# First loads of a two-layer decoder trunk spread over two DMA queues, small inputs packed, modulation products placed before the rotary angles

## The chip, the cores and the metric

One core of a Trainium2 chip runs the whole program. The metric is device time in microseconds for one execution. TensorE is called PE below, VectorE DVE, ScalarE ACT, GpSimd POOL, and SyncE SP; SP computes nothing here and only issues DMA transfers.

## The reference, cut to what matters

The kernel computes a decoder trunk of two layers on 256 tokens of width 1024. Layer 0 mixes tokens with multi-head latent attention with a rotary key, layer 1 with a block-sparse attention; each mixer is followed by a gated FFN. All six modulation vectors of a layer come from one vector c. What matters here is the very start:

```
ang = positions[..., None] * inv_freq ; cos, sin = cos(ang), sin(ang)
c_act = silu(c)
mod = (c_act @ mod_w[i] + mod_b[i]).reshape(B, 6, D)
hin = x * (1.0 + mod[:, 1]) + mod[:, 0]
proj = hin @ mla_w_in        # then q, k, v from proj; cos and sin turn the rotary parts
```

Before the first product of the mixer can run, a block of 128 features needs its shift and scale, that is two products of c_act with 1024x128 weights, and its part of x. Everything is float32.

## The kernel before, in words

Features lie on the 128 partitions, so x is held as z, 128 partitions by 8 blocks by 256 tokens. The modulation products aren't made on PE: `cb` holds c_act, repeated on every partition, and one VectorE instruction per half multiplies a 128x1024 slab of transposed modulation weights by it and sums along the row (`mod_half`, line 227). One unit of such weights is 1 MB and holds two halves; the first eight units (scale and shift of the first sub-layer for blocks j = 0 to 7) are loaded into tiles named `early`, the eighth into one named `raw`.

All DMA transfers are issued by SP, in one queue, in the order of lines 406 to 441: c (`cc`), the positions repeated on all partitions (`posi`), two constants of the rotary angles (`cst_sb`), modulation unit 0, the first two blocks of x, all small parameters (`par_sb`, 170 KB), a quarter of the mixer's input weights (`iraw`), unit 1, the other six blocks of x, the positions as a column (`posci`), and then the other units and quarters by turns. Unit 7 is loaded as two halves. The program keeps one completion counter for each of eight transfers in turn, so the issue of a transfer waits until the one eight places before it has landed.

The instructions of each engine run in the order in which the program writes them down (class `InOrder`). Around the change that order is: ACT takes exp(-c) (line 506), DVE finishes silu, PE transposes it eight times into PSUM (tile `cps`), ACT and DVE each copy a half to `cb` (lines 507 to 514). DVE then makes `kn2` from `par_sb` (line 552) and the first part of the rotary angles (`next(angles)`, line 564: `posb` from `posi`, `ang`, three steps on `n`). Then the loop of line 565 runs over the eight blocks j:

```
for n in range(2):
    mod_half(j, early[j], n)
...
V.tensor_add(gb0[:, :, j], modc[:, 0, 0:2, j], mb0[:, :, j])
A.activation(hin[:, j], z[:, j], AF.Identity, scale=..., bias=...)
A.mul(r[:, j], z[:, j], ALPHA)
for i in range(5): T.matmul(...)          # cqp, ckp, krp
...
next(angles, None)
```

In j = 0 four additions on `par_sb` are made, in j = 1 three products `lnx` and the copy `posc`; `next(angles, None)` makes one further part of the angles behind each of the first blocks. So PE's ten products of a block wait for ACT's `hin`, which waits for DVE's `gb0`. After the loop come the norms of the latents, the low-rank products (`wuqr`, `wuqn`, `wuk`, `wuv`), the heads and so on; from there PE works nearly without a gap, and DVE and ACT fill their idle time with splitting weights and with the remaining modulation units. What they fill in, and where, is decided while the program is built, by a model of the engines' times (class `Clock`), which also books each transfer on one data line in the order of the program.

Of the kernel before, what the change touches and what calls it, by code (L numbers as in the profile page):

```python
# [12 lines left out]
F32 = mybir.dt.float32  # L13
F32R = mybir.dt.float32r
BF16 = mybir.dt.bfloat16
I32 = mybir.dt.int32
AF = mybir.ActivationFunctionType
ALU = mybir.AluOpType
PSUM = bass.MemoryType.PSUM

P = 128
D = 1024
S = 256
NJ = D // P
# [6 lines left out]
ROPE_BASE = 10000.0  # L31
# [18 lines left out]
OFF_CB = OFF_CW + 2 * 3 * NF  # L50
OFF_QN = OFF_CB + 2 * NF
OFF_KN = OFF_QN + 2
NPAR = OFF_KN + 2

# [94 lines left out]
class InOrder:  # L151
# [6 lines left out]
    def __getattr__(self, name):  # L158
        f = getattr(self.engine, name)

        def call(*args, **kw):
            c = self.clock
            outs = [args[0]] + [kw[k] for k in ("accum_out",) if kw.get(k) is not None]
            ins = [a for a in list(args[1:]) + [v for k, v in kw.items() if k != "accum_out"] if hasattr(a, "ap")]
            size = math.prod(k for _, k in outs[0][:].ap)
            outs, ins = ([a[:] for a in x if a[:].tensor.name in c.written] for x in (outs, ins))
            if self.idle is not None:
                self.idle(c.ready(outs, ins))
            b = f(*args, **kw)  # L169
            if self.last is not None:  # L170
                self.tc.add_manual_dep(
                    b.ins, self.last.name,
                    mybir.DependencyInfo(mybir.DependencyClass.NoSync, mybir.DependencyReason.DATA),
                    reason="issue order")
            self.last = b.ins
            t = max(c.free[self.key], c.ready(outs, ins))
            if self.key == "Q":
                c.free["Q"] = t + 0.45
                c.run("D", max(c.free["Q"] + 0.65, c.free["D"]), size / 90e3, outs, ins, 1.0)
            else:  # L180
                c.run(self.key, t, c.cost(self.key, name, outs[0], ins), outs, ins)
            return b
        return call


@with_exitstack
def trunk_kernel(ctx: ExitStack, tc: tile.TileContext, xT, c_col, pos_row, pos_col, par, cst, mod,
                 w_mla_in, w_uqn, w_uqr, w_uk, w_uv, w_mla_o, w_qk, w_v, w_moba_o, w_f1, w_f2, out):
    nc = tc.nc
    clock = Clock()  # L190
    V, A, T, Q = (InOrder(tc, e, clock, k) for e, k in
                  ((nc.vector, "V"), (nc.scalar, "A"), (nc.tensor, "T"), (nc.sync, "Q")))
# [9 lines left out]
    one = ring("one", 1)  # L202
# [5 lines left out]
    psm = ring("psm", 3, space=PSUM)  # L208
# [8 lines left out]
    cb = one.tile([P, NJ, P], F32, name="cb")  # L217
# [179 lines left out]

    cc = one.tile([P, NJ], F32, name="cc")  # L400
    posi = tmp.tile([P, S], I32, name="posi", tag="t")
    posci = one.tile([P, 2], I32, name="posci")
    cst_sb = one.tile([P, 2], F32, name="cst_sb")
    par_sb = one.tile([P, NPAR], F32, name="par_sb")
    z = one.tile([P, NJ, S], F32, name="z")
    Q.dma_start(cc, c_col)
    Q.dma_start(posi, pos_row.to_broadcast([P, S]))
    Q.dma_start(cst_sb, cst)
    early, iraw = {}, {}

    def load_mod(j):
        if j < PIECES:
            early[j] = wts.tile([P, 2 * HALF], F32, name="early", tag="wx")
        else:
            early[j] = raws.tile([P, 2 * HALF], F32, name="raw", tag="raw")
        if j < NJ - 1:
            Q.dma_start(early[j], mod[j])
        else:
            for p in range(2):
                Q.dma_start(early[j][:, p * HALF:(p + 1) * HALF], mod[j][:, p])  # L420

    def load_in(k):
        iraw[k] = raws.tile([P, 2, 576], F32, name="iraw", tag="raw")
        Q.dma_start(iraw[k], w_mla_in[k])

    load_mod(0)
    Q.dma_start(z[:, 0:2], xT[:, 0:2])
    Q.dma_start(par_sb, par)
    load_in(0)
    load_mod(1)  # L430
    Q.dma_start(z[:, 2:8], xT[:, 2:8])
    Q.dma_start(posci, pos_col)
    load_mod(2)
    load_in(1)
    load_mod(3)
    load_mod(4)
    load_in(2)
    load_mod(5)
    load_mod(6)
    load_in(3)  # L440
    load_mod(7)

    def settled(li, pp):
        def still():
# [33 lines left out]
    ident = one.tile([P, P], F32, name="ident")  # L478
# [23 lines left out]
                        fill=MASKED, base=0, channel_multiplier=1)  # L502


    ce = one.tile([P, NJ], F32, name="ce")
    A.activation(ce, cc, AF.Exp, scale=-1.0)
    V.tensor_scalar(ce, ce, 1.0, None, op0=ALU.add)
    V.reciprocal(ce, ce)
    V.tensor_mul(ce, ce, cc)
    for hf in range(2):  # L510
        ps = psm.tile([P, 4, P], F32, name="cps", tag="mm")
        for j in range(4):
            T.transpose(ps[:, j], ce[:, 4 * hf + j:4 * hf + j + 1].to_broadcast([P, P]), ident)
        (A.copy if hf == 0 else V.tensor_copy)(cb[:, 4 * hf:4 * hf + 4], ps)


    hin = act.tile([P, NJ, S], F32, name="hin", tag="hh")
# [9 lines left out]
    def rotary():  # L527

        ang = tmp.tile([P, S], F32, name="ang", tag="g")
        V.tensor_copy(posb, posi)  # L530
        V.tensor_scalar(ang, posb, cst_sb[:, 0:1], None, op0=ALU.mult)
        for dst, turn, quarter in ((sin_t, 0.0, 0.0), (cos_t, 0.25, math.pi / 2)):
            n = tmp.tile([P, S], F32, name="n", tag="t")
            V.tensor_scalar(n, ang, INV_2PI, turn, op0=ALU.mult, op1=ALU.add)
            V.tensor_scalar(n, n, MAGIC, None, op0=ALU.add)
            V.tensor_scalar(n, n, MAGIC, None, op0=ALU.subtract)
            yield
            V.scalar_tensor_tensor(dst, n, -PI2_A, ang, op0=ALU.mult, op1=ALU.add)
            V.scalar_tensor_tensor(dst, n, -PI2_B, dst, op0=ALU.mult, op1=ALU.add)
            V.scalar_tensor_tensor(dst, n, -PI2_C, dst, op0=ALU.mult, op1=ALU.add)  # L540
            if quarter:
                V.tensor_scalar(dst, dst, quarter, None, op0=ALU.add)
            V.tensor_scalar(dst, dst, PI_SAFE, -PI_SAFE, op0=ALU.min, op1=ALU.max)
            A.activation(dst, dst, AF.Sin)
            yield
        A.mul(sin_t, sin_t, cst_sb[:, 1:2])
        table(AF.Abs_reciprocal_sqrt, cos_t)
        yield

    angles = rotary()  # L550
    kn2 = one.tile([P, 2], F32, name="kn2")
    V.tensor_scalar(kn2, par_sb[:, OFF_KN:OFF_KN + 2], -0.5, None, op0=ALU.mult)


    wuqr = act.tile([P, 2, 512], F32, name="wuqr", tag="k", bufs=1)
# [5 lines left out]
    Q.dma_start(wuqr, w_uqr)  # L561
    Q.dma_start(wuqn, w_uqn)
    mb0 = par_sb[:, OFF_MODB:OFF_MODB + 2 * NJ].rearrange("p (a j) -> p a j", a=2)
    next(angles)
    for j in range(NJ):
        k = j % 2
        raw = iraw[j // 2]
        if k == 0:
            krw = tmp.tile([P, 2, 2, 64], F32, name="krw", tag="krw", bufs=1)
            G.tensor_copy(krw, raw[:, :, 512:576].unsqueeze(2).to_broadcast([P, 2, 2, 64]))  # L570
        for n in range(2):
            mod_half(j, early[j], n)
        (wts if j < PIECES else raws).done.add(early[j][:].tensor.name)
        if j == 0:
            for li in range(2):
                for p_ in (1, 4):
                    V.tensor_scalar(modb(li, p_), modb(li, p_), 1.0, None, op0=ALU.add)
        if j == 1:
            lg = par_sb[:, OFF_LNG:OFF_LNG + 4 * NJ].rearrange("p (n j) -> p n j", n=4)
            lb = par_sb[:, OFF_LNB:OFF_LNB + 4 * NJ].rearrange("p (n j) -> p n j", n=4)  # L580
            V.tensor_scalar(lnx[:, 0], lb, ALPHA, None, op0=ALU.mult)
            V.tensor_scalar(lnx[:, 1], lg, -0.5 * ALPHA, None, op0=ALU.mult)
            V.tensor_scalar(lnx[:, 2], lg, -0.5, None, op0=ALU.mult)
        V.tensor_add(gb0[:, :, j], modc[:, 0, 0:2, j], mb0[:, :, j])
        A.activation(hin[:, j], z[:, j], AF.Identity, scale=gb0[:, 1, j:j + 1], bias=gb0[:, 0, j:j + 1])
        A.mul(r[:, j], z[:, j], ALPHA)
        for i in range(5):
            ps = cqp[:, i] if i < 2 else (ckp[:, i - 2] if i < 4 else krp)
            w = raw[:, k, i * P:(i + 1) * P] if i < 4 else krw[:, k].rearrange("p a b -> p (a b)")
            T.matmul(ps, w, hin[:, j], start=(j == 0 and i in (0, 2, 4)), stop=(j == NJ - 1 and i in (1, 3, 4)))  # L590
        if k == 1:
            raws.done.add(raw[:].tensor.name)
        if j == 1:
            V.tensor_copy(posc, posci)
        next(angles, None)
# [503 lines left out]
    for hf in range(2):  # L1099
        for t_ in range(2):  # L1100
            ps = psm.tile([P, 512], F32, name="vps", tag="mm")
# [123 lines left out]
    for hp in range(1, 4):  # L1225
        ps = project(vmm, v_loads[hp])
# [3 lines left out]
        a, b_ = heads[2 * hp - 2], heads[2 * hp - 1]  # L1230
# [7 lines left out]
        ps = project(qmm, qk_loads[2 * hp])  # L1238
# [12 lines left out]
    a, c = heads[6], heads[7]  # L1251
# [108 lines left out]
```

## Time and profile before

| | us |
|---|---|
| median of 3 runs (619.01 to 619.56) | 619.08 |
| the profiled execution, its own time | 619.66 |
| span of its profile | 617.8 |
| PE busy in the span | 591.9 (96%) |
| DVE busy | 484.3 (78%) |
| ACT busy | 365.8 (59%) |
| share of the 16 DMA engines, q1 | 65.7% |

The profiled execution took 1.9 us more than its span, which lies around the span at launch and end, and 0.6 us more than the median of the three runs. Times in the views are microseconds from the span's start. A line of the code says little here, because all engines' instructions are recorded at one line of the helper class; the tile's name tells which instruction it is. Instructions are written "out<-in".

### The profile page before, as it was taken

The numbers are of one execution on the slowest core, as the hardware profiler recorded it, in microseconds if no ns is written. First come the engines' busy times: TensorE is split into PE (matmuls) and PEld (weight loads), VectorE is DVE, ScalarE is ACT, GpSimd is POOL, SyncE is SP. The second block draws the span as 40 slices with busy tenths as digits, with TensorE's granted clock in tenths as the row PEclk, the third lists the DMA queues.
The fourth block names the chain that finished last, engine by engine and source line by source line (L and its number), as shares of the span: only waits on it lengthen the run. The fifth ranks groups of instructions, "written<-read, shape, count | busy, mean of one in ns | idle before, by whom it ended". The sixth has DMA issues, their size and how long they took to land.

```text
span 617.8 us, 11309 instructions
## 1 busy us (share of the span) xinstructions
PE 591.9 (96%) x4572; PEld 564.2 (91%) x4572; DVE 484.3 (78%) x937; ACT 365.8 (59%) x660; POOL 8.7 (1%) x27
## 2 busy tenths in 40 slices
PE   1799999999999999999999999999999999999994
PEld 1687579999999999999999999999999999999992
DVE  4976989799978898889788888478998765656545
ACT  1535686687753445555788777768676545454423
POOL 2000000000000000000000000000000000000000
PEclk9999999999999999999999999999999999999997
DMA  7999768357878888889247889423789755552001
GB/s 289 417 423 421 297 226 320 128 205 272 299 255 286 312 318 303 303 320 362 107 137 281 326 289 369 168 69 137 245 300 345 269 174 176 197 201 73 2 1 69
DMA packets 22373, 149.68 MB, mean 242 GB/s; under 512 B 2865, under 2 KB 3377, under 8 KB 4913
## 3 DMA queue, kind: packets, MB, share of 16 engines
q1 hardware_dynamic: 22320, 148.96, 65.7%
q8 instruction: 36, 0.59, 0.4%
q14 instruction: 17, 0.13, 0.1%
HBM read 147.90 MB, written 1.05 MB: 241 GB/s over the span
## 4 chain that ended last, share of the span: by engine, by line
PE 86%; DVE 8%; ACT 2%; DMA 1%; issue 1%; SPq 0%; POOLq 0%; ACTq 0%; DVEq 0%
PE abps L169 38%; PE ffy L169 19%; PE pps L169 10%; PE wops L169 7%; PE lrp L169 3%; DVE early L169 3%; PE fps L169 2%; DVE z L169 2%; PE sps L169 2%; PE po L169 1%; DMA par_sb<-in_par_dram 1%; PE vps L169 1%; ACT z L169 1%; DVE acc L169 1%; DVE raw L169 1%; PE swp L169 1%
## 5 line engine op out<-in xcount | busy, mean ns | idle before, releaser
L169 PE MATMUL abps<-nh,wx 128*128 128x256 f32 x1344 | 238.5, 280 | 0.5 <-DVE wx L169 0.5
L169 DVE TENSOR_TENSOR wx<-raw,wx 128x1024 fp32r<-128x1024 f32 x166 | 198.9, 1220 | 17.1 <-ACT wx L169 17.0
L169 PEld LDWEIGHTS abps<-nh,wx 128*128 128x128 f32 x1344 | 205.1, 188 | 1.1 <-DVE wx L169 1.0
L169 ACT CAST wx<-raw 128x1024 fp32r<-128x1024 f32 x166 | 170.5, 1045 | 36.3 <-PE ffy L169 18.0
L169 PE MATMUL abps<-nl,wx 128*128 128x256 f32 x672 | 188.0, 280 | 0.0
L169 PEld LDWEIGHTS abps<-nl,wx 128*128 128x128 f32 x672 | 126.3, 188 | 0.4
L169 PE MATMUL ffy<-gh,wx 128*128 128x256 f32 x704 | 126.0, 280 | 0.0
L169 PEld LDWEIGHTS ffy<-gh,wx 128*128 128x128 f32 x704 | 107.8, 188 | 0.0
L169 DVE SCALAR_TENSOR_TENSOR raw<-raw,cb 128x1024 f32<-128x1024 f32 x82 | 98.9, 1220 | 0.4 <-DMA raw<-in_mod_dram 0.4
L169 PE MATMUL ffy<-gl,wx 128*128 128x256 f32 x352 | 98.6, 280 | 0.0
L169 DVE SCALAR_TENSOR_TENSOR t<-abps,par_sb,t 128x255 f32<-128x255 f32 x84 | 40.5, 482 | 39.3 <-ACT t L169 37.8
L169 ACT ACTIVATE t<-abps,par_sb 128x256 f32<-128x256 f32 x42 | 23.6, 561 | 76.5 <-PE abps L169 76.5
L169 PEld LDWEIGHTS ffy<-gl,wx 128*128 128x128 f32 x352 | 66.1, 188 | 0.0
L169 PE MATMUL wops<-oh,wx 128*128 128x256 f32 x256 | 46.4, 283 | 0.0
L169 PE MATMUL pps<-nh,wx 128*128 128x256 f32 x224 | 41.3, 285 | 0.0
L169 PEld LDWEIGHTS wops<-oh,wx 128*128 128x128 f32 x256 | 39.3, 189 | 0.1
L169 PE MATMUL wops<-ol,wx 128*128 128x256 f32 x128 | 36.2, 282 | 0.3 <-DVE ol L169 0.3
L169 PEld LDWEIGHTS pps<-nh,wx 128*128 128x128 f32 x224 | 34.7, 188 | 0.3
L169 ACT ACTIVATE z<-z,st 128x128 f32<-128x128 f32 x64 | 27.1, 449 | 10.2 <-DVE st L169 10.0
L169 PE MATMUL pps<-nl,wx 128*128 128x256 f32 x112 | 31.3, 280 | 0.0
L169 DVE TENSOR_TENSOR g<-t,abps 128x256 f32<-128x256 f32 x42 | 17.6, 418 | 13.9 <-ACT t L169 13.8
L169 ACT ACTIVATE t<-t 128x256 f32<-128x256 f32 x44 | 18.3, 416 | 14.9 <-DVE t L169 13.7
(183 smaller groups left out, 692.9 us busy)
## 6 DMA issues: line engine op xcount, KB each, us to landing
raw<-in_w_f_dram SPq DMA_DIRECT2D x66, 1024.0 KB, 5.1
raw<-in_mod_dram SPq DMA_DIRECT2D x40, 1024.0 KB, 5.3
raw<-in_w_qk_dram SPq DMA_DIRECT2D x8, 1024.0 KB, 5.8
early<-in_mod_dram SPq DMA_DIRECT2D x7, 1024.0 KB, 12.7
raw<-in_w_mla_o_dram SPq DMA_DIRECT2D x4, 1024.0 KB, 7.6
raw<-in_w_v_dram SPq DMA_DIRECT2D x4, 1024.0 KB, 6.4
raw<-in_w_moba_o_dram SPq DMA_DIRECT2D x4, 1024.0 KB, 6.9
iraw<-in_w_mla_in_dram SPq DMA_DIRECT2D x4, 576.0 KB, 12.9
```

Of the source, the lines that this page charges most:

```text
L169: b = f(*args, **kw)
```

## The change

The first loads go out in two queues. ACT now issues `cc`, then (behind exp(-c), which is moved up to follow it) `par_sb`, the first two blocks of x, `posi` and the other six blocks of x. SP issues only the modulation units and the quarters of the input weights; unit 0 is now loaded as two halves, like unit 7. The two rotary constants and the column of positions have no transfers of their own any more: the host packs them into `par`, four columns longer. The transposes are written as one run of eight, and DVE's copy of its half of `cb` stands behind the definition of the angles, with no other VectorE instruction between. The call `next(angles)` ahead of the loop is gone, so that the first part of the angles is made at the end of block 0 and each later part one block later; `kn2` is made in block 1. The planner's clock books ACT's transfers as transfers.

```
 class InOrder, call():
-            if self.key == "Q":
-                c.free["Q"] = t + 0.45
-                c.run("D", max(c.free["Q"] + 0.65, c.free["D"]), size / 90e3, outs, ins, 1.0)
+            if name == "dma_start":
+                c.free[self.key] = t + 0.45
+                c.run("D", max(c.free[self.key] + 0.65, c.free["D"]), size / 90e3, outs, ins, 1.0)

-    posci = one.tile([P, 2], I32, name="posci")
-    cst_sb = one.tile([P, 2], F32, name="cst_sb")
     par_sb = one.tile([P, NPAR], F32, name="par_sb")
+    cst_sb = par_sb[:, OFF_ROT:OFF_ROT + 2]
+    posci = par_sb[:, OFF_POS:OFF_POS + 2].bitcast(I32)
     z = one.tile([P, NJ, S], F32, name="z")
-    Q.dma_start(cc, c_col)
-    Q.dma_start(posi, pos_row.to_broadcast([P, S]))
-    Q.dma_start(cst_sb, cst)
+    A.dma_start(cc, c_col)
+    ce = one.tile([P, NJ], F32, name="ce")
+    A.activation(ce, cc, AF.Exp, scale=-1.0)
+    A.dma_start(par_sb, par)
+    A.dma_start(z[:, 0:2], xT[:, 0:2])
+    A.dma_start(posi, pos_row.to_broadcast([P, S]))
+    A.dma_start(z[:, 2:8], xT[:, 2:8])

-        if j < NJ - 1:
+        if 0 < j < NJ - 1:
             Q.dma_start(early[j], mod[j])

-    load_mod(0)
-    Q.dma_start(z[:, 0:2], xT[:, 0:2])
-    Q.dma_start(par_sb, par)
-    load_in(0)
-    load_mod(1)
-    Q.dma_start(z[:, 2:8], xT[:, 2:8])
-    Q.dma_start(posci, pos_col)
-    load_mod(2)
-    load_in(1)
-    load_mod(3)
-    load_mod(4)
-    load_in(2)
-    load_mod(5)
-    load_mod(6)
-    load_in(3)
-    load_mod(7)
+    for k in range(4):
+        load_mod(2 * k)
+        load_in(k)
+        load_mod(2 * k + 1)

-    ce = one.tile([P, NJ], F32, name="ce")
-    A.activation(ce, cc, AF.Exp, scale=-1.0)
     V.tensor_scalar(ce, ce, 1.0, None, op0=ALU.add)
     V.reciprocal(ce, ce)
     V.tensor_mul(ce, ce, cc)
-    for hf in range(2):
-        ps = psm.tile([P, 4, P], F32, name="cps", tag="mm")
-        for j in range(4):
-            T.transpose(ps[:, j], ce[:, 4 * hf + j:4 * hf + j + 1].to_broadcast([P, P]), ident)
-        (A.copy if hf == 0 else V.tensor_copy)(cb[:, 4 * hf:4 * hf + 4], ps)
+    cps = [psm.tile([P, 4, P], F32, name="cps", tag="mm") for _ in range(2)]
+    for j in range(NJ):
+        T.transpose(cps[j // 4][:, j % 4], ce[:, j:j + 1].to_broadcast([P, P]), ident)
+    A.copy(cb[:, 0:4], cps[0])

     angles = rotary()
+    V.tensor_copy(cb[:, 4:8], cps[1])
     kn2 = one.tile([P, 2], F32, name="kn2")
-    V.tensor_scalar(kn2, par_sb[:, OFF_KN:OFF_KN + 2], -0.5, None, op0=ALU.mult)

-    next(angles)
     for j in range(NJ):
...
             V.tensor_scalar(lnx[:, 2], lg, -0.5, None, op0=ALU.mult)
+            V.tensor_scalar(kn2, par_sb[:, OFF_KN:OFF_KN + 2], -0.5, None, op0=ALU.mult)
```

The host code that feeds `cst` and `pos_col` now appends both to `par`.

## Rows read from the trace of the kernel before

**Rows 1.** Windows: time per engine, busy us (instructions), PE clock, DMA share, GB/s.
```profile
0.00:10.00 10.00, 1.94 (x8) 1.57 (x8) 1.50 (x4) 2.08 (x3) 2.97 (x17) 1.00 0.63 214
10.00:20.00 10.00, 4.51 (x11) 3.51 (x12) 9.48 (x32) 3.51 (x6) 0.53 (x1) 1.00 1.02 424
20.00:30.00 10.00, 7.19 (x31) 5.36 (x29) 9.76 (x21) 4.38 (x9) 0.55 (x1) 1.00 1.02 419
50.00:60.00 10.00, 10.00 (x44) 8.06 (x43) 4.70 (x10) 4.31 (x7) 0.00 (x0) 1.00 1.01 422
```

**Rows 2.** All waits of PE from 37.5 to 604 us.
```profile
PE abps L169 <- DVE wx L169: 0.5, 2, 0.3
PE wops L169 <- DVE ol L169: 0.3, 1, 0.3
PE cqp L169 <- ACT hin L169: 0.2, 1, 0.2
```

**Rows 3.** Chain that ended last, in order of time: start, us, what.
```profile
3.05 7.14 DMA par_sb<-in_par_dram
...
10.21 0.04 DVE kn L169
10.25 0.04 issue
10.29 0.30 DVE posb L169
...
11.87 2.57 DVE early L169 x4
14.44 0.30 DVE par_sb L169 x4
14.74 0.07 DVE gb L169
14.80 0.34 DVE sin_t L169
...
34.53 2.49 DVE raw L169 x4
37.02 0.02 issue
37.04 0.17 DVE gb L169
37.22 0.03 issue
37.24 0.61 ACT hin L169
```

**Rows 4.** Timeline, ACT and DVE up to `cb`, and the last half: start, us, engine, instruction.
```profile
0.73 1.28 ACT L169 ACT_TABLE_LOAD   x1 [0.73 <-PEq L1349]
2.34 0.21 ACT L169 ACTIVATE ce<-cc 128x8 f32<-128x8 f32 x1 [0.32 <-DMA cc<-in_c_col_dram]
4.73 0.59 ACT L169 COPY cb<-cps 128x512 f32<-128x512 f32 x1 [2.18 <-PE cps L169]
5.58 0.69 DVE L169 COPY cb<-cps 128x512 f32<-128x512 f32 x1 [2.12 <-PE cps L169]
35.59 1.41 DVE L169 SCALAR_TENSOR_TENSOR raw<-raw,cb 128x1024 f32<-128x1024 f32 x1
```

**Rows 5.** Timeline of SP: start, us, DMA issues.
```profile
0.74 0.37 SPq L169 DMA_DIRECT2D cc<-in_c_col_dram  x1
1.17 0.42 SPq L169 DMA_DIRECT2D posi<-in_pos_row_dram  x1
1.63 0.42 SPq L169 DMA_DIRECT2D cst_sb<-in_cst_dram  x1
2.10 0.43 SPq L169 DMA_DIRECT2D early<-in_mod_dram  x1
6.33 0.36 SPq L169 DMA_DIRECT2D early<-in_mod_dram  x1
18.60 1.75 SPq L169 DMA_DIRECT2D raw<-in_mod_dram  x2
22.50 0.33 SPq L169 DMA_DIRECT2D wuqr<-in_w_uqr_dram  x1
```

**Rows 6.** DMA issues: transfer, count, KB each, us from issue to landing (the single ones).
```profile
cc<-in_c_col_dram SPq DMA_DIRECT2D x1, 4.0 KB, 1.6
posi<-in_pos_row_dram SPq DMA_DIRECT2D x1, 128.0 KB, 4.1
cst_sb<-in_cst_dram SPq DMA_DIRECT2D x1, 1.0 KB, 4.7
early<-in_mod_dram SPq DMA_DIRECT2D x1, 1024.0 KB, 6.8
z<-in_xT_dram SPq DMA_DIRECT2D x1, 256.0 KB, 7.2
raw<-in_mod_dram SPq DMA_DIRECT2D x1, 512.0 KB, 15.3
```

**Rows 7.** DMA packets moved from 1.5 to 2.0 us and from 2.0 to 2.5 us.
```profile
DMA packets 144, 0.00 MB, mean 8 GB/s; under 512 B 144, under 2 KB 144, under 8 KB 144
DMA packets 25, 0.03 MB, mean 51 GB/s; under 512 B 0, under 2 KB 25, under 8 KB 25
```

More of the change, by code (lines that the diff above doesn't have):

```diff
@@ L52 @@
 OFF_KN = OFF_QN + 2
-NPAR = OFF_KN + 2
+OFF_ROT = OFF_KN + 2
+OFF_POS = OFF_ROT + 2
+NPAR = OFF_POS + 2
 IDLE = {"V": 0.45, "A": 0.5}
@@ L186, in trunk_kernel @@
 @with_exitstack
-def trunk_kernel(ctx: ExitStack, tc: tile.TileContext, xT, c_col, pos_row, pos_col, par, cst, mod,
+def trunk_kernel(ctx: ExitStack, tc: tile.TileContext, xT, c_col, pos_row, par, mod,
                  w_mla_in, w_uqn, w_uqr, w_uk, w_uv, w_mla_o, w_qk, w_v, w_moba_o, w_f1, w_f2, out):
@@ L1299 @@
                           cols(a["ffn_conv_b"]), cols(a["mla_q_norm"][0]), cols(a["mla_kv_norm"][0])], axis=1)
+    freq = (ROPE_BASE ** (-np.arange(32) / 32)).astype(np.float32)
+    cst = np.stack([np.tile(freq, 4), np.tile(np.repeat(np.array([1.0, -1.0], np.float32), 32), 2)], axis=1)
+    pos = np.ascontiguousarray(a["positions"].astype(np.int32).reshape(1, S))
+    par = np.concatenate([par, cst, np.ascontiguousarray(pos.reshape(2, P).T).view(np.float32)], axis=1)
     mw = a["mod_w"].reshape(2, D, 6, NJ, P)
@@ L1320 @@
     f2 = a["ffn_w_out"].reshape(2, NF // 2, 2, P, D).transpose(0, 1, 3, 2, 4).reshape(2, NF // 2, P, 2048)
-    freq = (ROPE_BASE ** (-np.arange(32) / 32)).astype(np.float32)
-    cst = np.stack([np.tile(freq, 4), np.tile(np.repeat(np.array([1.0, -1.0], np.float32), 32), 2)], axis=1)
-    pos = a["positions"].reshape(1, S)
     feeds = {
@@ L1329 @@
         "pos_row": pos,
-        "pos_col": pos.reshape(2, P).T,
         "par": par,
-        "cst": cst,
         "mod": np.stack(mods),
```

## The prediction

> **What bounds the kernel now.** I read the windows first, for the stage in which PE idles. Later, from 50 to 60 us, PE is busy all of the time [rows 1], and from 37.5 to 604 us all its waits for other engines come to 1.0 us in five pieces [rows 2]. So PE sets the pace once the loop over the eight blocks is over, and a microsecond won or lost before 37 us should reach the end whole. In the first 20 us PE works 6.45 us [rows 1].
>
> The chain of waits says what the beginning waits for [rows 3]. DVE's first instruction of it is kn2 at 10.21 us, released by the landing of par_sb, which was issued at 3.05 us and took 7.14 us. From there to 37.22 us the chain stays on DVE, which does sixteen modulation halves and the angles between them; ACT's last hin at 37.24 us then lets PE go. Its idle time ahead of that lies before 10.2 us: its own half of cb is ready at 5.58 + 0.69 = 6.27 us [rows 4], 3.9 us earlier.
>
> The DMA rows show a second chain of almost the same length. The first modulation unit is issued at 2.10 us and lands 6.8 us later, at 8.9 [rows 5, 6]. The last half unit is issued at 20.0 us (18.60 + 1.75 is the end of the second of two issues, and one alone takes 0.33) and lands 15.3 us later, at 35.3 [rows 5, 6]; DVE starts on it at 35.59 us, 1.65 us before hin [rows 3, 4]. Between 10 and 30 us the DMA engines are full, at 424 and 419 GB/s, but the first 10 us move only 2.14 MB [rows 1]. Data and DVE arrive together, so both must start earlier for the change to pay.
>
> **The change part by part.** The sum runs to the start of the last hin, 37.24 us before.
>
> *Work on DVE.* No compute instruction is added; kn2 and the first part of the angles only move. Let T be the moment at which posb can start. Behind it come 1.58 us up to the first half before (10.29 to 11.87), the rest behind gb of block 0 (14.80 to 37.24, 22.44 us), and kn2 in block 1, 0.08 us [rows 3]: the last hin starts at T + 24.1 us, and T = 13.1 would give the 37.24 us of before. T waits for two things: block 0's products and the landing of posi.
>
> *Block 0.* It needs cb and unit 0. On ACT the issue of cc now stands where the table load stood at 0.73 us; if the table load comes behind it, exp starts at 0.73 + 0.37 + 1.28 = 2.4 us instead of 2.34; if it comes ahead, cc is issued at 2.0 us instead of 0.74, 1.3 us later [rows 4, 5]. cc also shares the DMA engines now with unit 0, whose half of 512 KB takes 1.2 us at 424 GB/s, so it may land up to that much late. The ends are 0.1 and 1.3 us; I take 0.6, the middle, as no row is nearer to either. Then cb is ready at 6.9 us. Unit 0 is issued 1.36 us earlier, and nothing stands before it: before, its rows stood in the queue behind posi and the rotary constants, 129 KB that landed at 5.3 and 6.3 us [rows 5, 6]. Its first bytes can move when cc's did, from 1.7 us [rows 7], so 1.05 MB is there at 1.7 + 2.5 + 0.4 for the last receipt = 4.6 us. Block 0 therefore takes from 6.9 to 9.3 us (2.4 by the pair of raw), the four additions 0.30 and gb 0.07: ready for the angles at 9.7.
>
> *posi.* This is the new wait: in DVE's order it holds up the angles and everything behind them, units 1 to 7 included, for all engines. ACT issues par_sb, two blocks of x and posi behind exp, at about 3.2, 3.6 and 4.1 us, each some 0.45 us of issue like SP's [rows 5]; the issues end before ACT is wanted for cb at 4.73 + 0.6, so ACT's own queue costs nothing as long as none lasts beyond 0.8 us. When SP's queue would come into it: it issues unit 0, the first quarter (590 KB) and unit 1, and then waits for par_sb, since an issue waits for the transfer eight places ahead, as unit 2 did at 6.33 us, for the constants landing at 1.63 + 4.7 = 6.33 [rows 5, 6]. No row shows two queues at once, so I bound it. If bytes are shared evenly, the 0.57 MB of par_sb, x and posi need 2.7 us from 4.2: 7.3 with the receipt, no wait at all. If the queues take turns by whole transfers, unit 0, the quarter and unit 1 (2.69 MB) pass first, 3.26 MB in all: 1.7 + 7.7 + 0.4 = 9.8 us. If they take turns row by row, with equally many rows a transfer, three large transfers pass while ACT's three do, so unit 2 (1.05 MB) as well: 9.8 + 2.5 = 12.3, and 13.4 if cc is late too. The nearest row is the single queue, where x landed at 2.57 + 7.2 = 9.8 us, whole, directly behind unit 0 at 8.9: that is nearest to turns by transfer. I take 10.7, a third of the way to turns by row.
>
> The Trainium skill, "DMA: Bandwidth & Descriptors", section "Queues, rings and completion order", has each DMA engine take the rows of two queues in turn by packets, typically of some nine to seventeen descriptors. No run here shows that; a transfer of these would go out as one packet, and by it the posi figure would be 9.8 and the sum 0.9 us lower.
>
> *Data for the last block.* cc to the last half of unit 7 is 11,824 KB, 12.1 MB, 28.7 us at 422 GB/s. It ended at 35.3 us, as if it had begun at 6.6 at that rate. Starting at 1.7 it would land at 30.8; slow small rows, as in the windows before 10 us, may cost a little, so 31.5, bounds 30.8 and 33.9 (the earlier issue of 1.36 us alone). It is wanted 1.65 us ahead of hin, at 33.1 below: hidden. Two small transfers fewer, packing, and the split of unit 0 (one issue more, 0.43 us on SP, which has nothing to do then) cost nothing for the same reason. Latency of x isn't critical: its first blocks land by 10.4 at the latest of the middle cases, and only ACT waits for them.
>
> *Planner.* Its clock books transfers in another order, so pieces of weight splitting may move later on. PE's waits of 1.0 us in all [rows 2] bound the gain from it to that, and I allow 0.6 for a loss; I take 0.
>
> *Sum.* T = 10.7, the last hin at 34.8 instead of 37.24: 2.4 us less. The profiled execution's 619.66 us becomes 617.3; the median of the three runs lies 0.6 lower, and on it I forecast **616.7 us**.
>
> **The rivals.**
>
> *posi is early.* Queues share bytes evenly; then T = 9.3 to 9.7 and hin starts at 33.4 to 33.8, with the last half unit landing just in time. 3.4 to 3.8 less: 615.4. For it: x and posi are small. Against it: an 8 KB row of a unit and a 1 KB row of posi would have to be served as unlike numbers of rows.
>
> *Only the wait is exchanged.* Turns by row: posi lands at 12.3 to 13.4, T about 12.7, hin at 36.8. 0.4 less, 618.7: no change that can be measured. For it: SP always has large rows waiting; against it, SP's own stop behind par_sb.
>
> *Slower: posi last.* No gain is left from T = 13.1; each microsecond more is lost whole. posi reads one row of 1 KB for all partitions, and its rows moved at 25 in half a microsecond, where cc's 144 needed less than half of one [rows 7]: 128 of them spread over 1.5 us or more even alone, with 4.1 us to landing. If that slowness adds to turns by row, T is 13.4 + 1.5 = 14.9, and hin 39.0: 1.8 more, 620.8.
>
> *The data stay where they are.* The second queue moves nothing faster, and the last half lands at 33.9, by the earlier issue alone; hin is at 33.9 + 1.65 = 35.5, 1.7 less, 617.4. Beside this stands the Trainium skill, same page, section "Issuing engines are not separate DMA queues": it says that issuing from several engines saves issue time only. The full share of 1.02 from 10 us on agrees, the share of 0.63 before it leaves room [rows 1].
>
> **How the numbers follow.** A measurement of this kernel can tell about 0.2%, 1.24 us, from no change. The forecast, T from 9.9 to 11.9 and a gain of 1.3 to 3.3 us, has 0.43; posi early 0.15; the data bound 0.06; turns by row 0.25; slower 0.11. Faster is 0.43 + 0.15 + 0.06 = 0.64, the same 0.25, slower 0.11. The range takes the early case down to 615.0 and turns by row with the planner's loss up to 619.7. The likeliest case alone has 615.8 to 617.8.
>
> **What would show it.** Right: DVE starts block 0's first half at 6.3 to 7.6 us, the chain ahead of it goes through cc, exp and cb and no longer through par_sb; DVE then waits once, on posi, for about 1 us ahead of posb at 10.7; the last hin starts near 34.8; the last half unit lands by 32 us; PE's waits after that stay near 1 us. It is wrong if DVE waits for posi beyond 12 us, or not at all; if it waits for a modulation unit (early or raw) in the blocks 1 to 7; if cb is later than 7.6 us, for a late cc or ACT held in its issues; or if PE loses behind the loop what was won in it.

## The result, and the profile of the changed kernel

The changed kernel is slower: 624.55 us in the median of four runs (624.35 to 625.78) against 619.29 (619.01 to 619.56) for the kernel before on the same chip, 5.26 us, a ratio of 1.0094 with an interval of 1.0082 to 1.0106. The profiled execution took 624.35 us with a span of 622.6; before it was 619.66 with 617.8, 4.8 us less.

The chain that ended last shows where the time went. First its shares of the whole span, by engine, from the page; then pieces of its beginning in order of time (start, us, what):

```profile
PE 86%; DVE 8%; DMA 3%; ACT 2%; issue 1%; ACTq 0%; POOLq 0%; DVEq 0%
```

```profile
0.73 3.59 DMA cc<-in_c_col_dram
4.35 0.21 ACT ce L171
...
4.72 0.70 ACTq L171
...
5.45 12.69 DMA posi<-in_pos_row_dram
...
19.83 2.28 DVE early L171 x4
...
39.60 2.49 DVE raw L171 x4
42.31 0.61 ACT hin L171
```

Before, the beginning of the chain was the landing of par_sb at 10.2 us, and the last hin started at 37.24 [rows 3]. Now it is cc, exp (`ce`), ACT's issues, and then 12.69 us of waiting for posi, issued at 5.45. The last hin starts at 42.31, 5.07 us later. PE behind it is as it was; its waits for other engines from 42.5 us to the end of the stages are these (engine and line, waited for: us in total, times, longest), where before they came to 1.0 [rows 2]:

```profile
PE abps L171 <- DVE wx L171: 0.6, 2, 0.3
PE wops L171 <- DVE ol L171: 0.3, 1, 0.3
PE cqp L171 <- ACT hin L171: 0.2, 1, 0.2
```

So the loss lies ahead of 42.3 us. In the timeline of that stretch (start, us, engine, instruction, and in brackets the idle time ahead and what ended it):

```profile
4.35 0.21 ACT L171 ACTIVATE ce<-cc 128x8 f32<-128x8 f32 x1 [1.89 <-DMA cc<-in_c_col_dram]
4.35 0.34 ACTq L171 DMA_DIRECT2D par_sb<-in_par_dram  x1
...
5.45 0.56 ACTq L171 DMA_DIRECT2D posi<-in_pos_row_dram  x1
...
7.32 0.69 DVE L171 COPY cb<-cps 128x512 f32<-128x512 f32 x1 [2.12 <-PE cps L171]
...
8.11 1.22 DVE L171 SCALAR_TENSOR_TENSOR early<-early,cb 128x1024 f32<-128x1024 f32 x1
...
11.92 0.39 DVE L171 TENSOR_SCALAR par_sb<-par_sb 128x8 f32<-128x8 f32 x4 [1.35 <-DMA par_sb<-in_par_dram]
...
18.16 0.29 DVE L171 CAST posb<-posi 128x256 f32<-128x256 int32 x1 [5.79 <-DMA posi<-in_pos_row_dram]
```

exp, which needed cc, ran at 2.34 us before [rows 4]; it now runs at 4.35, and ACT issues the three small transfers behind it. DVE makes block 0's products from 8.11, waits 1.35 us for par_sb and then 5.79 us for posi. Everything of blocks 1 to 7 stands behind posb in DVE's order.

The issues show how long each transfer took (count, KB each, us from issue to landing); posi took 4.1 us before, cc 1.6 [rows 6]:

```profile
z<-in_xT_dram ACTq DMA_DIRECT2D x1, 256.0 KB, 9.8
par_sb<-in_par_dram ACTq DMA_DIRECT2D x1, 172.0 KB, 7.5
posi<-in_pos_row_dram ACTq DMA_DIRECT2D x1, 128.0 KB, 12.7
cc<-in_c_col_dram ACTq DMA_DIRECT2D x1, 4.0 KB, 3.6
```

Packets moved by each queue tell why (q1 is SP's queue, q10 ACT's; packets, MB, share of 16 engines). A packet is one row of a transfer here, or a few bytes that end one: of the 943 from 7.95 to 18.16 us, 96 are under 512 bytes. The stretches are 1.5 to 4.35 us (cc beside unit 0), 4.35 to 7.95 (par_sb issued, hardly a row of it moved), and from there to the landing of par_sb at 11.9, of x at 14.5 and of posi at 18.16:

```profile
q1 hardware_dynamic: 212, 0.80, 83.7%
q10 hardware_dynamic: 144, 0.00, 2.8%
...
q1 hardware_dynamic: 287, 1.38, 100.1%
q10 hardware_dynamic: 3, 0.00, 0.3%
...
q1 hardware_dynamic: 184, 1.38, 84.2%
q10 hardware_dynamic: 174, 0.24, 16.5%
...
q1 hardware_dynamic: 159, 0.72, 68.9%
q10 hardware_dynamic: 155, 0.24, 25.3%
...
q1 hardware_dynamic: 131, 0.94, 66.4%
q10 hardware_dynamic: 140, 0.33, 23.5%
```

In the last three stretches together SP's queue moves 474 packets and ACT's 469: one for one. SP's carry 3.03 MB, ACT's 0.81. That is what ACT's small rows pay: beside each of them passes a row of up to 8 KB. They don't come in bursts either. From 8.35 to 9.15 us, while par_sb passes, the counts are just as even, about two packets of each queue for each of the 16 engines:

```profile
q1 hardware_dynamic: 33, 0.27, 83.4%
q10 hardware_dynamic: 31, 0.04, 14.2%
```

The windows show that the DMA engines did gain something, 302 GB/s in the first ten microseconds against 214 [rows 1], and gave part of it back while posi's rows moved (time per engine, then PE clock, DMA share, GB/s):

```profile
0.00:10.00 10.00, 1.94 (x8) 1.57 (x8) 3.12 (x7) 2.08 (x3) 4.61 (x18) 1.00 0.81 302
10.00:20.00 10.00, 4.63 (x10) 3.20 (x10) 2.72 (x13) 0.91 (x2) 0.71 (x1) 1.00 0.95 380
...
14.00:15.00 1.00, 0.00 (x0) 0.00 (x0) 0.00 (x0) 0.37 (x1) 0.00 (x0) 1.00 0.77 240
15.00:16.00 1.00, 0.72 (x2) 0.63 (x3) 0.00 (x0) 0.53 (x2) 0.00 (x0) 1.00 0.73 271
```

### The profile page after: what moved, and what is told of

It reads as the page before. It is cut to its first block, busy times and chain, and to the rows that moved or that the text cites. A ratio compares the mean times of both kernels' runs of the same rounds, so it can differ in the third digit from the quotient of the medians.

```text
span 622.6 us, 11305 instructions
## 1 busy us (share of the span) xinstructions
PE 593.6 (95%) x4572; PEld 565.6 (91%) x4572; DVE 483.9 (78%) x937; ACT 365.7 (59%) x660; POOL 11.2 (2%) x27
## 3 DMA queue, kind: packets, MB, share of 16 engines
HBM read 147.90 MB, written 1.05 MB: 239 GB/s over the span
## 4 chain that ended last, share of the span: by engine, by line
PE 86%; DVE 8%; DMA 3%; ACT 2%; issue 1%; ACTq 0%; POOLq 0%; DVEq 0%
PE abps L171 38%; PE ffy L171 19%; PE pps L171 10%; PE wops L171 7%; PE lrp L171 3%; DVE early L171 2%; PE fps L171 2%; DMA posi<-in_pos_row_dram 2%; DVE z L171 2%; PE sps L171 2%; PE po L171 1%; PE vps L171 1%; DVE acc L171 1%; ACT z L171 1%; DVE raw L171 1%; PE swp L171 1%
## 5 line engine op out<-in xcount | busy, mean ns | idle before, releaser
L171 DVE SCALAR_TENSOR_TENSOR t<-abps,par_sb,t 128x255 f32<-128x255 f32 x84 | 40.4, 481 | 39.0 <-ACT t L171 37.5
L171 ACT ACTIVATE z<-z,st 128x128 f32<-128x128 f32 x64 | 27.1, 449 | 10.2 <-DVE st L171 10.0
L171 ACT ACTIVATE t<-t 128x256 f32<-128x256 f32 x44 | 18.3, 415 | 14.5 <-DVE t L171 13.4
## 6 DMA issues: line engine op xcount, KB each, us to landing
early<-in_mod_dram SPq DMA_DIRECT2D x6, 1024.0 KB, 11.9
```

## The experiments

The theory after this reading: ACT's queue moves one row for each row of SP's, so its small transfers crawl, posi as the last of three needed ones worst, and DVE waits for it in order. The rivals: ACT issues too late, behind exp; ACT's queue is slow by itself; posi is slow because all partitions read one row; the new order of DVE's work costs the time. Each ratio is against the kernel before, run on the same chip: its median was 618.83 us beside order_only, issue_first, half_rows and small_first, 618.74 beside posi_rows, hold_unit1, small_rows and one_queue, and 618.81 beside the other four.

**Only DVE's order (order_only).** The kernel before, its single queue untouched:

```
     kn2 = one.tile([P, 2], F32, name="kn2")
-    V.tensor_scalar(kn2, par_sb[:, OFF_KN:OFF_KN + 2], -0.5, None, op0=ALU.mult)
...
-    next(angles)
...
             V.tensor_scalar(lnx[:, 2], lg, -0.5, None, op0=ALU.mult)
+            V.tensor_scalar(kn2, par_sb[:, OFF_KN:OFF_KN + 2], -0.5, None, op0=ALU.mult)
```

> The kernel before, one queue and all its loads, with only VectorE's order of the change: block 0's products in front of the first part of the angles, kn2 in block 1. Theory 1 (turns by row: the two queues give each other one row for one row, so each of ScalarE's small transfers costs eight of SyncE's 8 KB rows, and posi, third behind par_sb and x, comes at 18 us): the new order is harmless by itself; block 0 starts when unit 0 lands, about 8.9 us, the last half unit still lands near 35.3, so the last hin is at 36.9 and the time 618.9, the same. Theory 2 (the order is the cause): DVE then waits somewhere behind block 0 and the time is 621 to 625.

Measured: 618.74 us, ratio 0.9998 (0.9989 to 1.0007). The order costs nothing and brings nothing there, though posb can start at 10.92 us: block 0 waits 1.99 us for unit 0, and units 1 and 3 are late by 0.93 and 0.42. The last hin starts at 36.64.

**ACT issues ahead of exp (issue_first).** The changed kernel with exp moved behind ACT's five issues:

```
     A.dma_start(cc, c_col)
-    ce = one.tile([P, NJ], F32, name="ce")
-    A.activation(ce, cc, AF.Exp, scale=-1.0)
     A.dma_start(par_sb, par)
...
     A.dma_start(z[:, 2:8], xT[:, 2:8])
+    ce = one.tile([P, NJ], F32, name="ce")
+    A.activation(ce, cc, AF.Exp, scale=-1.0)
```

> The changed kernel with exp(-c) behind ScalarE's five DMA issues instead of behind the first, so that par_sb, x and posi are issued from 1.2 us instead of 4.35. Theory 1 (turns by row): they meet unit 0 in 4 KB rows and the quarter in 4.6 KB rows, posi meets unit 1; it lands near 10.8, block 0's products end at the same time, the last hin is at 35.2 and the time is about 617.5. Theory 3 (ScalarE's queue needs a fixed time of 3 us and more for each transfer, whatever SyncE moves): cc 4.4, par_sb 8, x 11.5, posi 15, the last hin at 39.2, 621.4.

Measured: 619.67 us, ratio 1.0013 (1.0003 to 1.0022). From its timeline:

```profile
2.13 0.48 ACTq L171 DMA_DIRECT2D posi<-in_pos_row_dram  x1
...
11.84 0.29 DVE L171 CAST posb<-posi 128x256 f32<-128x256 int32 x1 [0.48 <-DMA posi<-in_pos_row_dram]
...
14.68 1.23 DVE L171 SCALAR_TENSOR_TENSOR early<-early,cb 128x1024 f32<-128x1024 f32 x1 [1.17 <-DMA early<-in_mod_dram]
```

posi is issued 3.3 us earlier and lands 6.3 us earlier, because the issue wins itself and with it a place beside fewer large rows. So the wait behind exp is a large part of the loss. But posi still takes 9.7 us, and the gain ends at the next thing that is late, unit 1: the kernel isn't faster than before. The expected time was missed by 2 us: posi landed 1.0 us later than expected, and unit 1 costs the 1.17.

**Smaller rows on SP's side (half_rows).** Units 0 to 3 as halves, so that SP's rows are 4 KB, everything else as changed:

```
-        if 0 < j < NJ - 1:
+        if 3 < j < NJ - 1:
             Q.dma_start(early[j], mod[j])
```

> The changed kernel with units 0 to 3 loaded as halves in 4 KB rows, where it was unit 0 alone; ScalarE's transfers unchanged. Theory 1 (turns by row): each of ScalarE's transfers now costs eight 4 KB rows, 1.7 to 1.9 us instead of 3 to 3.6, so posi lands near 13.5 instead of 18.2, the last hin is at 37.7 instead of 42.3, and the time is about 620. Theory 3 (fixed time for each transfer): posi stays near 18 and the time near 624.5.

Measured: 620.94 us, ratio 1.0034 (1.0023 to 1.0045). ACT's queue is issued as late as in the changed kernel, and par_sb lands at 11.2, x at 13.2, posi at 14.8 us: 2.0 and 1.6 us apart, where the changed kernel has 2.6 and 3.7. The issues:

```profile
z<-in_xT_dram ACTq DMA_DIRECT2D x1, 256.0 KB, 8.4
par_sb<-in_par_dram ACTq DMA_DIRECT2D x1, 172.0 KB, 6.8
posi<-in_pos_row_dram ACTq DMA_DIRECT2D x1, 128.0 KB, 9.3
```

Nothing of ACT's own was touched; the small transfers follow the size of the rows beside them. That shows turns by row. Between the landings of par_sb and x the two queues move 162 packets to 160; only the end of posi, from 13.5 us on, has less beside it, as SP's queue is running out there. It was expected to land at 13.5: par_sb's first rows moved only 4.2 us after its issue.

**Small ones first in SP's queue (small_first).** The packing and DVE's order of the change, but cc, par_sb and x in SP's queue, ahead of or right behind unit 0, and posi alone in ACT's, issued first:

```
-    A.dma_start(cc, c_col)
+    Q.dma_start(cc, c_col)
+    A.dma_start(posi, pos_row.to_broadcast([P, S]))
+    Q.dma_start(par_sb, par)
...
-    A.dma_start(par_sb, par)
-    A.dma_start(z[:, 0:2], xT[:, 0:2])
-    A.dma_start(posi, pos_row.to_broadcast([P, S]))
-    A.dma_start(z[:, 2:8], xT[:, 2:8])
...
     for k in range(4):
         load_mod(2 * k)
+        if k == 0:
+            Q.dma_start(z[:, 0:2], xT[:, 0:2])
         load_in(k)
         load_mod(2 * k + 1)
+        if k == 0:
+            Q.dma_start(z[:, 2:8], xT[:, 2:8])
```

> The changed kernel with its packing and its order on VectorE, but cc, par_sb and x back in SyncE's queue (cc, par_sb, unit 0, two blocks of x, quarter, unit 1, six blocks of x, the rest); ScalarE's queue has posi alone, issued first. Theory 1 (turns by row): posi meets only the small rows of cc and par_sb and the first rows of unit 0 and lands by 6; cb is ready at 6.3 to 6.9, block 0 ends at 9.3, nothing waits for posi, the last hin is at 33.4 to 34 and the time 615.4 to 616, faster than both kernels. Theory 3 (a fixed lateness of ScalarE's queue): posi lands later than 9.5 and the time is 618 or more.

Measured: 617.78 us, ratio 0.9981 (0.9971 to 0.9990). It is the fastest of all and beats both kernels, the one before by 1.05 us. posi lands at 4.9 us, and posb starts at 9.64, which is what the prediction had for a posi that isn't late (9.7). But the chain up to the last hin runs over the data now (start, us, what):

```profile
5.95 12.41 DMA iraw<-in_w_mla_in_dram
...
18.38 15.92 DMA raw<-in_mod_dram
...
34.32 1.29 DVE raw L171 x2
...
35.83 0.61 ACT hin L171
```

Units 1 and 3 are late by 1.21 and 0.41 us, and the last half lands at 34.30, when DVE is ready for it at 34.26. The miss of some 2 us against what was expected is this. Its windows from 1 to 5 us say where the data lose:

```profile
1.00:2.00 1.00, 0.00 (x0) 0.00 (x0) 0.00 (x0) 0.83 (x1) 0.96 (x5) 1.00 0.09 17
2.00:3.00 1.00, 0.00 (x0) 0.00 (x0) 0.00 (x0) 0.46 (x1) 0.99 (x5) 1.00 0.43 103
3.00:4.00 1.00, 0.00 (x0) 0.00 (x0) 0.51 (x3) 0.21 (x1) 0.54 (x2) 1.00 0.74 161
4.00:5.00 1.00, 0.79 (x4) 0.82 (x5) 0.07 (x1) 0.00 (x0) 0.00 (x0) 1.00 0.92 254
```

**posi from 128 rows of its own (posi_rows).** The changed kernel, with the host laying the positions out 128 times:

```
-    A.dma_start(posi, pos_row.to_broadcast([P, S]))
+    A.dma_start(posi, pos_row)
...
-        "pos_row": pos,
+        "pos_row": np.broadcast_to(pos, (P, S)),
```

> The changed kernel with the positions laid out by the host as 128 equal rows, so that posi reads 128 different rows of HBM instead of one row 128 times; same bytes, same queue, same place. If reading one address slows posi and what is beside it: DMA's rate no longer falls to 240 to 270 GB/s while posi is moved, posi lands at 17.3 instead of 18.2 us, the time is about 623.6. If turns by row alone made posi late: posi at 18.2, 624.5.

Measured: 623.33 us, ratio 1.0071 (1.0054 to 1.0088). posb starts at 16.89 instead of 18.16. Reading one row for all partitions costs 1.3 us of the 5, and no more. The slow stretch at 14 to 16 us, 240 and 271 GB/s in the changed kernel, is gone:

```profile
14.00:15.00 1.00, 0.00 (x0) 0.00 (x0) 0.00 (x0) 0.46 (x1) 0.00 (x0) 1.00 1.09 422
15.00:16.00 1.00, 0.81 (x2) 0.71 (x3) 0.00 (x0) 0.45 (x2) 0.00 (x0) 1.00 1.03 418
```

**SP held behind the first quarter (hold_unit1).** Unit 1, and with it all that SP issues later, waits until ACT has written eight elements into its tile, which the transfer overwrites:

```
-    for k in range(4):
+    load_mod(0)
+    load_in(0)
+    early[1] = wts.tile([P, 2 * HALF], F32, name="early", tag="wx")
+    A.copy(early[1][:, 0:NJ], cc)
+    Q.dma_start(early[1], mod[1])
+    for k in range(1, 4):
```

> The changed kernel, but SyncE may issue unit 1 and all behind it only once ScalarE has written a few elements into unit 1's tile behind its own five issues (about 6.8 us; they are overwritten). Only unit 0 and the first quarter, 1.64 MB, are then ahead when par_sb is issued at 4.35. Theory 1b (ScalarE's rows are made up behind the transfers that SyncE issued before them, and come only when most of those have moved): the first rows of par_sb move at about 5.4 instead of 7.9 us, par_sb lands near 6.5, x near 7.5, posi near 9.5; no wait for posi, the last hin at 35.2 to 36.2 (data), 617.5 to 618.4. Theory 4 (ScalarE's queue starts its rows some 3.5 us behind an issue in any case): first rows at 7.9, posi at 12.5 to 13, the last hin at 37, 619.3.

Measured: 620.93 us, ratio 1.0035 (1.0022 to 1.0048). par_sb's rows begin about 1.95 us after the issue, between what the two theories expected, when SP's rows are nearly through, and it lands at 7.46; x lands at 9.6. posi lands at 12.3 although from 7 to 10 us ACT's queue is alone; from 8 to 10 it moves 117 packets, at 122 and 159 GB/s. And the delay is found the other way round: SP issues unit 1 at 6.41 us, and its first packets, three, move between 10 and 11, behind most of what ACT had issued. Unit 1 is 2.70 us late for it, so the time itself says little.

**SP held earlier still (hold_half).** The same hold behind unit 0's first half, so that SP has nothing left to move when ACT issues:

```
-    for k in range(4):
+    early[0] = wts.tile([P, 2 * HALF], F32, name="early", tag="wx")
+    Q.dma_start(early[0][:, 0:HALF], mod[0][:, 0])
+    A.copy(early[0][:, HALF:HALF + NJ], cc)
+    Q.dma_start(early[0][:, HALF:2 * HALF], mod[0][:, 1])
+    load_in(0)
+    load_mod(1)
+    for k in range(1, 4):
```

> As hold_unit1, but already the second half of unit 0 and all behind it wait for ScalarE, so that SyncE's queue is empty when par_sb is issued near 4.35 us. If par_sb's rows start late only because of what SyncE issued before them (2.0 us after the issue in hold_unit1, 3.6 in the changed kernel): they start 1.0 to 1.4 us after the issue, as cc's did. If ScalarE's queue has a lateness of its own: 1.9 us or more. The time is not of interest; unit 0 is late, 621 to 623.

Measured once, 622.4 us; it was run for the packets. From 5 to 6 us and from 6 to 7:

```profile
q10 hardware_dynamic: 145, 0.19, 74.8%
...
q10 hardware_dynamic: 158, 0.26, 102.0%
```

par_sb is issued at 4.23 us, its rows begin about 0.9 us later, and it lands at 6.5, 2.3 us after the issue instead of 7.5. ACT's queue isn't slow by itself. The delay until the first rows grows with what SP issued before it: 0.9 us with nothing left, 1.95 with part of a unit and a quarter, 3.6 in the changed kernel. It isn't bytes alone: with halved rows it is 4.2 us, though SP moves as much meanwhile, 1.35 MB against 1.38, in 347 packets instead of 287.

**The second queue without the new order (queues_only).** The changed kernel with the one call put back:

```
     mb0 = par_sb[:, OFF_MODB:OFF_MODB + 2 * NJ].rearrange("p (a j) -> p a j", a=2)
+    next(angles)
     for j in range(NJ):
```

> The changed kernel with the first part of the angles back in front of block 0's products, as before: only the two queues and the packing are left of the change (and kn2's place). Theory 1 (posi late through its queue): VectorE now waits for posi at 18.2 us with block 0's products (2.9 us) still to do behind it, so the last hin is near 45.2 and the time 627.3; the new order was the part of the change that helped. Theory 2 (the order costs): 621 or less.

Measured: 627.56 us, ratio 1.0142 (1.0127 to 1.0157). In its timeline the one wait is the whole story:

```profile
19.02 0.29 DVE L171 CAST posb<-posi 128x256 f32<-128x256 int32 x1 [10.99 <-DMA posi<-in_pos_row_dram]
```

So with the second queue the new order of DVE's work saves 3 us: it fills part of the wait with block 0.

**posi ahead of par_sb and x (posi_first).** The changed kernel with one issue moved:

```
+    A.dma_start(posi, pos_row.to_broadcast([P, S]))
     A.dma_start(par_sb, par)
     A.dma_start(z[:, 0:2], xT[:, 0:2])
-    A.dma_start(posi, pos_row.to_broadcast([P, S]))
```

> The changed kernel with posi in front of par_sb and x in ScalarE's queue. Theory 1 (each of ScalarE's transfers pays its own turns against SyncE's rows): posi lands near 12, par_sb near 15.3, x near 18.3; VectorE waits for par_sb instead (its four additions stand in front of the angles), posb starts at 15.7, the last hin is at 39.8, the time 622. If the place in the queue does not matter: 624.5.

Measured: 621.77 us, ratio 1.0047 (1.0031 to 1.0064). posi lands at 12.4 us, and now par_sb is late:

```profile
14.82 0.39 DVE L171 TENSOR_SCALAR par_sb<-par_sb 128x8 f32<-128x8 f32 x4 [4.22 <-DMA par_sb<-in_par_dram]
...
15.19 0.28 DVE L171 CAST posb<-posi 128x256 f32<-128x256 int32 x1
```

par_sb, now second, lands 2.9 us later than in the changed kernel, and posi itself still takes 8.0 us: each transfer in this queue pays, whatever its place.

**Packing and order in the single queue (pack_only).** The kernel before with the constants packed into `par`, the run of eight transposes and the new order; cc, posi, unit 0, x, par_sb and so on stay in SP's queue in that order.

> The kernel before with only the packing and the change's order on VectorE: one queue, two transfers of 1 KB fewer. Without the constants' transfer, unit 0 lands about 0.7 us earlier than in order_only (8.2), the last half unit at 34.3 to 34.6; the last hin at 36 to 36.3, the time 617.9 to 618.3: a fast version, and the second queue is then all of the change's loss. If the second queue was not the cause: 622 or more.

Measured: 619.16 us, ratio 1.0004 (0.9995 to 1.0013), the last hin at 37.09. The time expected, 617.9 to 618.3, wasn't reached, but without the second queue the change is neutral. (Unit 0 isn't split here either; in small_first it is, and that kernel isn't slower.) So the second queue is the whole loss.

**Two attempts at the small_first order without its slow start.** small_rows is small_first with the 128 rows of posi as above; one_queue puts these rows too into SP's queue and makes the first part of the angles ahead of cb:

```
-    A.dma_start(posi, pos_row.to_broadcast([P, S]))
+    Q.dma_start(posi, pos_row)
...
+    next(angles)
     V.tensor_copy(cb[:, 4:8], cps[1])
```

> small_first (cc, par_sb and x in SyncE's queue, posi alone on ScalarE's) with the positions laid out as 128 different rows. If reading one address held back the first 5 us (17, 103, 161 and 254 GB/s in small_first from 1 to 5 us): the rate is above 350 GB/s from 3 us on, the last half unit lands at 32 instead of 34.3, the last hin is at 33.5 to 34, the time 615.5. If not: 617.8 as in small_first.

> Everything in SyncE's queue in the order cc, positions as 128 different rows, par_sb, unit 0, two blocks of x, quarter, unit 1, six blocks of x, the rest; the first part of the angles stands in front of VectorE's copy to cb, where VectorE idles. If the second queue has no use of its own: cc at 2.4, angles 3.5 to 5.1, block 0 from 6.3, the last half unit at 31.5, the last hin at 32.5 to 33.2, the time 614.4 to 615, the fastest. If a second queue is worth something: slower than small_rows.

Measured: 619.24 us, ratio 1.0004 (0.9995 to 1.0013), and 619.21 us, 1.0007 (0.9998 to 1.0016). Both missed by some 4 us. The profiled execution of small_rows was the fastest of its ten (617.88, the last hin at 36.30) and that of one_queue the slowest (620.12, 37.90), so their traces differ no more than runs of one kernel do. posi is there by 3.5 us in both, but the rate from 3 to 8 us is 245 to 348 GB/s in the one and 234 to 348 in the other; unit 1 is 2.23 us late in small_rows, and five units are late in one_queue, by 0.58 to 1.92 us. So the slow start isn't only posi's reading of one row. What else causes it stays open.

## Why the prediction was wrong

**The bound was right.** PE carries the shift whole: the last hin moved by 5.07 us and the median by 5.26. **The sum over DVE's work was right too:** the last hin at T + 24.1. With T read from each trace the formula gives 42.26 for the changed kernel (42.31 measured), 40.99 for posi_rows (40.93), 38.9 for half_rows (38.84) and 39.29 for posi_first (39.21); for issue_first 37.11 with the 1.17 us of unit 1 added (37.14).

**The step that failed is posi's landing**, T = 10.7, where 18.16 was measured. The mechanism named for it (one new wait, in DVE's order, ahead of everything) is the one that happened; the size of the wait was wrong, beyond even the slow rival's 14.9. Three of its assumptions were off:

- *The issue.* ACT was to issue par_sb at 3.2 us; it did at 4.35. cc was allowed 1.3 us of delay at most and had 2.0. I counted the bytes of unit 0 that might pass first; but cc is 128 rows of 32 bytes, and its queue's 144 packets took turns with 212 of SP's.
- *The start.* I let par_sb's rows move about as soon as they were issued. They began 3.6 us later, at 7.95, behind 1.38 MB that SP's queue moved meanwhile. hold_half, with 0.9 us, shows that this is the price of what SP has issued by then, not of ACT's queue.
- *The turns.* I took turns by whole transfers as nearest and went a third of the way to turns by row. The counts are one for one. From 7.95 to 18.16 the two queues moved 3.84 MB, which at a full rate of 418 GB/s takes 9.2 us; the loss of speed at 14 to 16 us, 0.33 MB short of the full rate, is 0.8 more, and the sum is within 0.3 us of the 10.2 measured.

The rival "only the wait is exchanged" had turns by row, and "posi last" added the slow reading of one row, which posi_rows puts at 1.3 us against its 1.5. Both counted the turns from 1.7 us, as if ACT's rows had been there from the beginning. With the right mechanism and the wrong start they were 3 to 6 us short.

The Trainium skill, "DMA: Bandwidth & Descriptors", section "Queues, rings and completion order", lets a DMA engine drain a packet of some nine to seventeen descriptors from one queue before it switches. The counts here, 184 to 174, 159 to 155 and 131 to 140, are even, and still even (33 to 31) within 0.8 us of the 3.95 in which par_sb passed: bursts of nine rows and more don't show. x and posi shrink with SP's rows in half_rows. All this fits turns of one row where the rows are of 1 to 8 KB; the measurement decides.

**The data step failed as well**, though unseen in the result. I had the last half unit land at 31.5, with 33.9 as the worst; in the changed kernel it landed at about 34 (issued in the 0.91 us from 22.91, 10.4 us to landing), where DVE reached it only at 40.66. The full rate doesn't begin at 1.7 us: the first ten microseconds move 2.14 MB before, 3.02 in the changed kernel, of which the slow stretch at 14 to 16 takes part back, and 2.60 in small_first. By 20 us both are 0.44 MB ahead of before, 1.05 us at 420 GB/s, and that is the whole gain of the data: 35.3 becomes 34.2, and 34.30 in small_first. So by this estimate even a posi in time would have put the last hin at 34.2 + 1.65 = 35.9, not 34.8: a gain of 1.4 us instead of 2.4. small_first, with 35.83 and 617.78 us, comes nearest to that case. The rival "the data stay where they are" had this bound, at 35.5.

The Trainium skill's other rule, same page, section "Issuing engines are not separate DMA queues", says that issuing from a second engine saves issue time alone. The traces agree: by 20 us the changed kernel has moved as much as small_first, where all but posi goes through one queue. They add a price: the second queue also gave up the order of the transfers.

**What held besides:** packing and the order of DVE's work cost nothing that can be told (the ratios of order_only and pack_only are 0.9998 and 1.0004), and the planner's moves cost nothing that can be seen (PE's waits of 1.1 us against 1.0). Block 0 started at 8.11, beyond the 6.3 to 7.6 given, for cc's delay; the wait for par_sb at 11.92 wasn't foreseen, but is hidden by posi's.

## What to carry to other kernels

What follows rests on this one kernel. A small transfer that is needed early belongs ahead of the large ones in the same queue, or, if it must go alone, into a second queue before the first has issued anything large; beside rows of 8 KB each of its small rows paid for one of them here. Don't put its issue behind a computation that itself waits for a transfer. And before pricing a new order of loads, ask at which rate the first microseconds move bytes at all: here that set what an order could gain.

## What the runs showed of the hardware that was not expected

- Two queues on one set of DMA engines took turns by row: 474 packets to 469 over 10.2 us, 33 to 31 within 0.8.
- Rows of the queue that issued later began 0.9 to 4.2 us after their issue, 0.9 with nothing of the other queue left and 3.6 to 4.2 while about 1.4 MB of it moved; in hold_unit1 it was SP's that came 4 us late. What holds them wasn't settled.
- 128 KB of posi, read from one row for all partitions, lowered the rate to 240 and 271 GB/s in the changed kernel and came with 122 and 159 in hold_unit1, where no other queue moved; from 128 rows of its own the same two microseconds moved 422 and 418, and it landed 1.3 us sooner.
- The eight completion counters are shared by both queues: in the changed kernel SP's issues waited 3.8 us for par_sb, 6.3 for x and 2.5 for posi, all ACT's transfers. It cost nothing that can be seen: DVE waited for no modulation unit there.
